# Where a kernel sums its modulation weights, how its weight splits are ranked, and when its attention heads begin

## The chip, the cores and the metric

One NeuronCore of one Trainium2 chip runs the whole program. The metric is device microseconds of one execution, from the first to the last instruction plus what lies around them; smaller is better. PE is the matmul engine, DVE the vector engine, ACT the scalar engine, POOL the general one and SP the engine whose queue issues nearly all DMAs here.

## The reference, cut to what matters

Two transformer blocks run one after the other on 256 tokens of width 2048, all in float32. The second block is modulated: six vectors of 2048 come from a matrix `w_mod` of 2048 x 12288 and one conditioning vector `c`, and they shift, scale and gate the second block only.

```python
def second_block(x, c, w_mod, b_mod, ...):
    mod = silu(c) @ w_mod + b_mod
    sh1, sc1, g1, sh2, sc2, g2 = split(mod, 6)
    h = rmsnorm_2(x, attn_norm_g) * (1.0 + sc1) + sh1
    ...                                       # w_in, two attentions, w_out
    x = x + g1 * (mix @ w_out)
    h = rmsnorm_2(x, mlp_norm_g) * (1.0 + sc2) + sh2
    u = relu(h @ w_ff1)
    x = x + g2 * ((u * u) @ w_ff2)
    return rmsnorm_2(x, final_norm_g)
```

The first block (`first_block`) is: norm, `w_in`, three kinds of attention heads, `w_out`; norm, a gated feed-forward net with `w_gate`, `w_up`, `w_down`; norm, and a small gated embedding with `w_ple_gate` and `w_ple_proj`. Nothing of it needs `mod`.

## The kernel before

**Stages.** `build` runs them in order: `mixer1` (w_in and the heads of the first block), `out_proj1` (w_out), `conv_ffn` (gate, up, down, then `ple_values`), `ple`, `mixer2` and `out_proj2` (second block's attention), `mlp2` (ff1 and ff2). In the profiled execution DVE's first weight split of `out_proj1` is at about 352 us, of `conv_ffn` at 448, of `ple` at 1170, of `mixer2` at 1251 and of `mlp2` at 1492; the first three are called the first three stages below.

**Weights.** Each weight matrix is streamed once in blocks of 512 KB. `prep` (L283) loads a block into `raw` (4 buffers), makes `whi`, its rounded part, on ACT (L291) and `wlo`, the remainder, on DVE (L292); `whi` and `wlo` have 3 buffers each. Every product is three matmuls: `linear` (L328 to L330) has the weights moving, `linear_t` (L370 to L372) has them standing still. After each block `tick` (L260) lets waiting pieces of other work go on: `spawn` starts a generator, whose `yield n` means "go on n blocks later"; `jobs` holds attention heads that begin as ticks allow.

**Modulation sums.** `w_mod` has 96 rows of 128 outputs, each summed in two halves, so 192 halves. `mod_half` (L920) loads half a row block, 512 KB, into one of two `wmod` buffers and multiplies and sums it on DVE (L930) with `cact`, the activated vector `c`. The load may not be issued ahead of the newest weight load (`issue_after`). `tick` calls it `mod_rate` times per block: 0.36 after the first block column of w_in. `mod_upto(80)` at the end of `conv_ffn` issues what is left of the first 160 halves at once. The last 32 halves, which make `g2`, are done in `mlp2`: there a second `mod_open` loads and activates `c` again, the rate is 1.0, and `mod_upto(96)` and `mod_row` (a transpose, a store and a spread back over the partitions) stand ahead of the fifth ff1 chunk.

**Order of the work.** The program is traced once; a list scheduler then fixes the order of each engine's instructions by priority (the place in the trace) and by readiness in its own cost model. On the chip each engine runs its instructions in that fixed order and waits at each for its inputs. `high_priority()` gives what is traced inside it rank 0, ahead of everything ordinary. `prep` uses it, and so do the last column's evacuation in `ple` (`urgent`) and most of `mod_norm`.

**The two modulated norms.** `mod_norm(i, ss)` (L1104) runs for each half i of the tokens when the last column of `ple` or of `out_proj2` is evacuated: row sums, a power on POOL (`rstd_tile`), four scalings `hn` (L1113), then transposes on PE, scale and shift `z`, and a split into `xt`. Around it, blocks of weights are held in a group: the last blocks of the old matrix run for both halves of the tokens out of tiles such as `whiaaaaa`, the first ones of the new matrix out of `whibbbb` (`seq_out`, `seq_in`). The three single blocks after such a first group take the three `whi`/`wlo` buffers.

**Heads.** In `mixer1`, `qkv` transposes q and k (L653), evacuates them into `qT` (L658, L660) and then appends the heads that are complete to `jobs` (L620). `head` (L768) begins with its score matmuls (L783, L785).

Of the kernel before, what the change touches and what calls it, by code (L numbers as in the profile page):

```python
# [9 lines left out]
F32 = mybir.dt.float32  # L10
# [4 lines left out]
ALU = mybir.AluOpType  # L15
# [6 lines left out]
CW = 512  # L22
# [199 lines left out]
class K:  # L222
    def __init__(self, ctx, tc, a, out):
        self.ctx, self.tc, self.nc, self.a, self.out = ctx, tc, tc.nc, a, out
        self.uid = 0
        self.pend = []
        self.jobs = []
        self.job_every = 0.0
        self.job_acc = 0.0
        self.mod_rate = 0.0  # L230
        self.mod_acc = 0.0
        self.done = set()

    def n(self, s):
        self.uid += 1
# [47 lines left out]
    def prep(self, src, ncol, hold=None, shift=False):  # L283
        nc = self.nc
        pool, n, k = (self.HOLD, len(hold), hold) if hold else (self.W, 3, "")
        with self.tc.high_priority():
            raw = self.t(self.W, [P, 1024], "raw", 4)
            self.wdma = nc.sync.dma_start(raw[:, :ncol], src)
            e, s = (0, 0) if hold else (64, 16 * shift)
            hi, lo = (self.t(pool, [P, 1024 + e], w + k, n, F32R)[:, s:s + 1024] for w in ("whi", "wlo"))  # L290
            nc.scalar.activation(hi[:, :ncol], raw[:, :ncol], AF.Copy)  # L291
            nc.vector.tensor_tensor(lo[:, :ncol], raw[:, :ncol], hi[:, :ncol].bitcast(F32), op=ALU.subtract)  # L292
        return hi, lo

    def load(self, dst, src):
# [11 lines left out]
    def linear(self, xt, name, seq, off, cw, evac, before=None):  # L307


        nc = self.nc  # L310
        left, ps = {}, {}
        for c, b in seq:
            for i in range(2):
                left[c, i] = left.get((c, i), 0) + (len(b) if isinstance(b, tuple) else 1)
        started = set()

        def products(c, b, i, w):
            st = (c, i) not in started
            started.add((c, i))
            left[c, i] -= 1  # L320
            en = left[c, i] == 0
            sl = slice(i * P, (i + 1) * P)
            o = ps[c][i][:, :cw]
            for j in range(2):
                xh, xl = xt(2 * b + j)
                wh = moving(w[0][:, j * cw:(j + 1) * cw])
                wl = moving(w[1][:, j * cw:(j + 1) * cw])
                nc.tensor.matmul(o, xh[:, sl], wh, start=st and j == 0, stop=False)  # L328
                nc.tensor.matmul(o, xh[:, sl], wl, start=False, stop=False)  # L329
                nc.tensor.matmul(o, xl[:, sl], wh, start=False, stop=en and j == 1)  # L330
            return en

        for c, b in seq:
            if c not in ps:
                ps[c] = [self.ps.tile([P, 512], F32, name=self.n("mm"), tag="mm", bufs=4) for _ in range(2)]
            group = b if isinstance(b, tuple) else (b,)
            for b1 in group:
                if before is not None:
                    before(c, b1)
            src = [self.wblock(name, off(c) + b1 * 2 * P * cw, 2, cw) for b1 in group]  # L340
            if len(group) == 1:
                w = self.prep(src[0], 2 * cw)
                for i in range(2):
                    if products(c, b, i, w):
                        evac(c, i, ps[c][i])
                self.tick()
                continue
            ws = [self.prep(x, 2 * cw, ("a" if group[0] else "b") * len(group)) for x in src]
            for i in range(2):
                for n, b1 in enumerate(group):  # L350
                    if products(c, b1, i, ws[n]):
                        evac(c, i, ps[c][i])
                    if n % 2 == 1 or n == len(group) - 1:
                        self.tick()
# [78 lines left out]
    def build(self, stop=None):  # L433
        ctx, tc, nc, a = self.ctx, self.tc, self.nc, self.a
        self.C = self.pool(ctx, "C")
        self.W = self.pool(ctx, "W")
        self.X = self.pool(ctx, "X")
        self.DR = self.pool(ctx, "DR", bass.MemoryType.DRAM)
        self.ps = self.pool(ctx, "ps", bass.MemoryType.PSUM)
        C = self.C  # L440
        self.h = self.t(C, [P, 2, D], "h")
        self.ident = self.t(C, [P, P], "ident")
        self.gains = self.t(C, [P, NG], "gains")
        self.mhalf = self.t(C, [P, 16], "mhalf")
        self.macc = self.t(C, [P, 96, 2], "macc")
        self.modT = self.t(C, [P, 96], "modT")
        self.mhalves = 0
        nc.vector.memset(self.mhalf, -0.5)
        self.G = lambda nme, k=0, w=1: self.gains[:, GOFF[nme] + k:GOFF[nme] + k + w]
        self.mixctx = mixctx = ExitStack()  # L450
        modctx = ExitStack()
        self.modctx = modctx
        Y = self.pool(mixctx, "Y")
        self.mix = self.new_xt(Y, "mix", 8)
        self.MOD = self.pool(modctx, "MOD", side="right")
        with ExitStack() as s:
            self.mixer1(s)
            if stop == "mix":
                self.flush()
                return  # L460
            self.out_proj1()
        mixctx.close()
        if stop == "out1":
            self.flush()
            return
        with ExitStack() as s:
            self.ple_open(s)
            self.conv_ffn()
            if stop == "ffn1":
                self.flush()  # L470
                return
            self.mod_upto(80)
            modctx.close()
            self.holdctx = ExitStack()
            self.HOLD = self.pool(self.holdctx, "HOLD", side="right")
            self.ple()
        if stop == "blk1":
            self.flush()
            return
        with ExitStack() as s:  # L480
            self.mixer2(s)
            if stop == "mix2":
                self.flush()
                return
            self.out_proj2()
        if stop == "out2":
            self.flush()
            return
        self.mlp2()


    def mixer1(self, s):
        nc, a, tc, G = self.nc, self.a, self.tc, self.G
# [175 lines left out]
        for ci, (kind, h0, parts) in enumerate(W_IN_CHUNKS):  # L669
            off = ci * D * CW  # L670
            if kind == "a1":
# [35 lines left out]
                if ci == 0:  # L707
                    def before(c, b):
                        load_x(c, b)
                        if b == 5:  # L710
                            load_h()
                        if b == 7:
                            consts()
                    self.chunk(xg, "w_in", off, KT, CW, evac, before)
                    self.mod_rate = 0.36
                else:
                    self.chunk(xg, "w_in", off, KT, CW, evac)
            elif kind == "a2":
# [48 lines left out]

    def head(self, fam, h, kt, q, k, v, cst):  # L768
        nc, M = self.nc, self.M
        extra = None  # L770
        if fam == "f":
            lh = self.t(M, [P, T], "lh", 2)
# [7 lines left out]
        for i in range(2):  # L780
            o = S[:, 0:P] if i == 0 else S[:, P:384]
            n = P if i == 0 else T
# [10 lines left out]
        hi, lo = self.mix[kt // 4]  # L793
# [309 lines left out]

    def mod_norm(self, i, ss):  # L1104
        nc = self.nc
        rs = self.rstd_tile(ss, i)
        if i == 0:
            self.xn.extend(self.new_xt(self.X, "xt", 8))
        hns = []
        for c in range(4):  # L1110
            hn = self.t(self.HOLD, [P, CW], "hn", self.hnb)
            with self.tc.high_priority():
                nc.vector.tensor_scalar(hn, self.h[:, i, c * CW:(c + 1) * CW], rs, None, op0=ALU.mult)  # L1113
            hns.append(hn)
        yield 2
        sl = slice(i * P, (i + 1) * P)
        for c in range(4):
            pt = self.transpose4(hns[c])
            z = self.t(self.HOLD, [P, 4, P], "z", 2)
            for j in range(4):  # L1120
                k = 4 * c + j
                g, b = self.mgs[:, k:k + 1], self.msh[:, k:k + 1]
# [291 lines left out]
    def mlp2(self):  # L1414
        nc = self.nc
        with ExitStack() as s:
            F = self.pool(s, "F2")
# [3 lines left out]
            ss = self.t(F, [P, 64], "ssf")[:, :2 * NCH + 2].rearrange("p (i c) -> p i c", i=2)  # L1421
# [60 lines left out]
            pend = None  # L1482
            for g in range(4):
                for n in range(4):
                    if g == 1 and n == 0:
                        self.mod_upto(96)
                        self.spawn(self.mod_row([g2], 80, F, 5))
                    ff1(4 * g + n)
                    if g == 0 and n == 0:
                        self.holdctx.close()  # L1490
                        R = self.MOD = self.pool(s, "F3", side="right")
                        self.mod_open(None)
                        g2 = self.t(R, [P, D], "grow")
                        self.mod_rate = 1.0
                    if n == 0 and pend is not None:
                        ff2(pend, False)
                pend = list(range(4 * g, 4 * g + 4))
# [30 lines left out]
```

## Time and profile before

| | us |
|---|---|
| median of 3 runs | 2221.02 |
| lowest and highest | 2218.52, 2226.48 |
| the profiled execution, its own time | 2216.61 |
| span of the profiled execution | 2214.8 |
| granted TensorE clock, mean | 0.995 |

The profile shows one execution: busy time per engine, the waits with what ended them, the chain of work that ended last, and the granted clock, of which 1.00 is 2.4 GHz and 0.5 is 1.2 GHz. A matmul is shown until its modelled end, so PE is at its peak only where the count of matmuls per stretch is at its highest as well: about 360 of the `linear_t` kind or 187 of the `linear` kind in 40 us.

### The profile page before, as it was taken

The numbers are of one execution on the slowest core, as the hardware profiler recorded it, in microseconds if no ns is written. First come the engines' busy times: TensorE is split into PE (matmuls) and PEld (weight loads), VectorE is DVE, ScalarE is ACT, GpSimd is POOL, SyncE is SP. The second block draws the span as 40 slices with busy tenths as digits, with TensorE's granted clock in tenths as the row PEclk, the third lists the DMA queues.
The fourth block names the chain that finished last, engine by engine and source line by source line (L and its number), as shares of the span: only waits on it lengthen the run. The fifth ranks groups of instructions, "written<-read, shape, count | busy, mean of one in ns | idle before, by whom it ended". The sixth has DMA issues, their size and how long they took to land.

```text
span 2214.8 us, 34936 instructions
## 1 busy us (share of the span) xinstructions
PE 2153.0 (97%) x13714; PEld 1966.8 (89%) x13714; DVE 1567.7 (71%) x2329; ACT 1102.2 (50%) x1560; POOL 25.8 (1%) x35
## 2 busy tenths in 40 slices
PE   9999999999999999999999899998989999999998
PEld 7788887899998999989988789888878998998997
DVE  7877776877887687767777766768775555555555
ACT  6655554544454454444455555556434444444444
POOL 0000000000000000000000000000000000000000
PEclk9999999999999999999999999999999999999999
DMA  8665666777777777777778743656886666666664
GB/s 321 226 219 200 209 235 219 250 254 256 272 268 271 271 264 271 271 268 276 269 266 311 246 145 125 185 184 213 300 307 219 200 199 202 199 199 202 200 200 162
DMA packets 147537, 517.82 MB, mean 234 GB/s; under 512 B 17115, under 2 KB 21292, under 8 KB 146860
## 3 DMA queue, kind: packets, MB, share of 16 engines
q1 hardware_dynamic: 147228, 515.58, 68.8%
q8 instruction: 107, 1.75, 0.3%
q14 instruction: 58, 0.48, 0.1%
q10 hardware_dynamic: 144, 0.01, 0.0%
HBM read 513.38 MB, written 2.14 MB: 233 GB/s over the span
## 4 chain that ended last, share of the span: by engine, by line
PE 62%; DMA 7%; issue 6%; DVE 3%; ACT 1%; SPq 0%; POOL 0%; ACTq 0%; POOLq 0%; DVEq 0%
PE mm L372 10%; PE mm L371 10%; PE mm L370 10%; PE mm L330 9%; PE mm L328 9%; PE mm L329 9%; DMA wmod<-in_w_mod 6%; DVE wlo L292 2%; PE aux L392 0%; DMA raw<-in_w_ff 0%; PE aux L760 0%; PE aux L1285 0%; DVE wmod L930 0%; ACT whi L291 0%; PE aux L1236 0%
## 5 line engine op out<-in xcount | busy, mean ns | idle before, releaser
L291 ACT ACTIVATE whi<-raw 128x1024 fp32r<-128x1024 f32 (+1 forms) x746 | 783.2, 1051 | 908.3 <-PE mm L330 495.5
L292 DVE TENSOR_TENSOR wlo<-raw,whi 128x1024 fp32r<-128x1024 f32 (+1 forms) x746 | 902.2, 1215 | 366.9 <-ACT whi L291 365.8
L372 PE MATMUL mm<-xt,wlo 128*128 128x256 f32 x2368 | 653.1, 276 | 8.7 <-DVE wlo L292 8.5
L371 PE MATMUL mm<-xt,whi 128*128 128x256 f32 x2368 | 651.4, 275 | 0.0
L370 PE MATMUL mm<-xt,whi 128*128 128x256 f32 x2368 | 651.3, 275 | 0.0
L372 PEld LDWEIGHTS mm<-xt,wlo 128*128 128x128 f32 x2368 | 454.5, 192 | 11.5 <-DVE wlo L292 11.3
L371 PEld LDWEIGHTS mm<-xt,whi 128*128 128x128 f32 x2368 | 454.6, 192 | 0.2
L370 PEld LDWEIGHTS mm<-xt,whi 128*128 128x128 f32 x2368 | 454.6, 192 | 0.2
L930 DVE SCALAR_TENSOR_TENSOR wmod<-wmod,cact 128x1024 f32<-128x1024 f32 x192 | 234.9, 1223 | 181.0 <-DMA wmod<-in_w_mod 180.3
L329 PE MATMUL mm<-wlo,hid 128*128 128x512 f32 x848 | 322.4, 380 | 1.2 <-DVE wlo L292 1.2
L328 PE MATMUL mm<-whi,hid 128*128 128x512 f32 x848 | 322.5, 380 | 0.0
L330 PE MATMUL mm<-whi,hid 128*128 128x512 f32 x848 | 322.3, 380 | 0.0
L329 PE MATMUL mm<-wlo,xt 128*128 128x512 f32 (+2 forms) x660 | 250.0, 379 | 5.9 <-DVE wlo L292 5.6
L328 PE MATMUL mm<-whi,xt 128*128 128x512 f32 (+2 forms) x660 | 252.5, 383 | 1.2 <-ACT whi L291 1.2
L330 PE MATMUL mm<-whi,xt 128*128 128x512 f32 (+2 forms) x660 | 248.3, 376 | 0.0
L329 PEld LDWEIGHTS mm<-wlo,hid 128*128 128x128 f32 x848 | 160.7, 190 | 25.3 <-DVE wlo L292 2.7
L330 PEld LDWEIGHTS mm<-whi,hid 128*128 128x128 f32 x848 | 160.7, 189 | 22.7
L328 PEld LDWEIGHTS mm<-whi,hid 128*128 128x128 f32 x848 | 160.6, 189 | 22.6 <-DVE t L1438 0.2
L329 PEld LDWEIGHTS mm<-wlo,xt 128*128 128x128 f32 x660 | 124.8, 189 | 27.1 <-DVE wlo L292 11.8
L328 PEld LDWEIGHTS mm<-whi,xt 128*128 128x128 f32 x660 | 124.8, 189 | 17.5 <-ACT whi L291 1.7
L330 PEld LDWEIGHTS mm<-whi,xt 128*128 128x128 f32 x660 | 124.8, 189 | 15.2
L329 PE MATMUL mm<-wlo,mix 128*128 128x512 f32 x244 | 93.0, 381 | 1.9 <-DVE wlo L292 1.9
(349 smaller groups left out, 1790.6 us busy)
## 6 DMA issues: line engine op xcount, KB each, us to landing
raw<-in_w_ff SPq DMA_DIRECT2D x256, 512.0 KB, 4.3
wmod<-in_w_mod SPq DMA_DIRECT2D x192, 512.0 KB, 5.3
raw<-in_w_in SPq DMA_DIRECT2D x120, 512.0 KB, 4.6
raw<-in_w_gate SPq DMA_DIRECT2D x88, 512.0 KB, 4.5
raw<-in_w_up SPq DMA_DIRECT2D x88, 512.0 KB, 4.6
raw<-in_w_down SPq DMA_DIRECT2D x88, 512.0 KB, 4.3
raw<-in_w_out SPq DMA_DIRECT2D x64, 512.0 KB, 3.8
raw<-in_w_pg SPq DMA_DIRECT2D x32, 512.0 KB, 4.8
```

Source lines behind the costliest of these rows:

```text
L291: nc.scalar.activation(hi[:, :ncol], raw[:, :ncol], AF.Copy)
L292: nc.vector.tensor_tensor(lo[:, :ncol], raw[:, :ncol], hi[:, :ncol].bitcast(F32), op=ALU.subtract)
L328: nc.tensor.matmul(o, xh[:, sl], wh, start=st and j == 0, stop=False)
L329: nc.tensor.matmul(o, xh[:, sl], wl, start=False, stop=False)
L330: nc.tensor.matmul(o, xl[:, sl], wh, start=False, stop=en and j == 1)
L370: nc.tensor.matmul(o, hi[:, ws], xh, start=first, stop=False, skip_group_check=True)
L371: nc.tensor.matmul(o, hi[:, ws], xl, start=False, stop=False, skip_group_check=True)
L372: nc.tensor.matmul(o, lo[:, ws], xh, start=False, stop=(b == last and j == 1), skip_group_check=True)
L930: nc.vector.scalar_tensor_tensor(raw, raw, 1.0, self.cact[:, us], op0=ALU.mult, op1=ALU.mult, accum_out=self.macc[:, j, u:u + 1])
```

## The change

Four things are changed. The rate of the modulation sums in the first three stages goes from 0.36 to 0.5 per block, `conv_ffn` ends with `mod_upto(96)`, and everything of them goes out of `mlp2`; `mod_row` for `g2` is started after the first ff1 chunk. The weight splits of `prep` get a rank 2000 places ahead of where they are traced in place of rank 0, and the row sums and the power of `mod_norm` get rank 0. The `wlo` splits of the three single blocks behind a first group are queued on DVE behind the last `hn` of half 0. And `head` yields once ahead of its score matmuls.

```diff
     def prep(self, src, ncol, hold=None, shift=False):
-        with self.tc.high_priority():
+        with self.tc.high_priority(offset=min(2000, self.tc.cur_priority)):
             ...
-            nc.vector.tensor_tensor(lo[:, :ncol], raw[:, :ncol], hi[:, :ncol].bitcast(F32), op=ALU.subtract)
+            with self.tc.issue_after(self.behind.ins) if self.behind is not None else nullcontext():
+                nc.vector.tensor_tensor(lo[:, :ncol], raw[:, :ncol], hi[:, :ncol].bitcast(F32), op=ALU.subtract)
     def linear(...):
+        ring = 0
             if len(group) == 1:
+                self.behind = self.normed if ring > 0 else None
+                ring -= 1
                 w = self.prep(src[0], 2 * cw)
+                self.behind = None
             ...
             ws = [self.prep(x, 2 * cw, ("a" if group[0] else "b") * len(group)) for x in src]
+            ring = 0 if group[0] else 3
     def build(...):
-            self.mod_upto(80)
+            self.mod_upto(96)
     def mixer1(...):
-                    self.mod_rate = 0.36
+                    self.mod_rate = 0.5
     def head(self, fam, h, kt, q, k, v, cst):
         nc, M = self.nc, self.M
+        yield 1
     def mod_norm(self, i, ss):
-        rs = self.rstd_tile(ss, i)
+        with self.tc.high_priority():
+            rs = self.rstd_tile(ss, i)
             ...
-                nc.vector.tensor_scalar(hn, self.h[:, i, c * CW:(c + 1) * CW], rs, None, op0=ALU.mult)
+                op = nc.vector.tensor_scalar(hn, self.h[:, i, c * CW:(c + 1) * CW], rs, None, op0=ALU.mult)
+            if i == 0:
+                self.normed = op
     def mlp2(self):
-                    if g == 1 and n == 0:
-                        self.mod_upto(96)
-                        self.spawn(self.mod_row([g2], 80, F, 5))
                     ff1(4 * g + n)
                     if g == 0 and n == 0:
                         self.holdctx.close()
-                        R = self.MOD = self.pool(s, "F3", side="right")
-                        self.mod_open(None)
+                        R = self.pool(s, "F3", side="right")
                         g2 = self.t(R, [P, D], "grow")
-                        self.mod_rate = 1.0
+                        self.spawn(self.mod_row([g2], 80, F, 3))
```

## Rows read from the trace of the kernel before

**Rows 1.** The page, part 1: busy us, share of the span, instructions.
```profile
PE 2153.0 (97%) x13714; PEld 1966.8 (89%) x13714; DVE 1567.7 (71%) x2329; ACT 1102.2 (50%) x1560; POOL 25.8 (1%) x35
```
**Rows 2.** Stretches: us, busy of PE, PEld, DVE, ACT, POOL, clock, DMA, GB/s.
```profile
448.00:1160.00 712.00, 708.78 (x5332) 678.10 (x5331) 540.57 (x685) 336.08 (x370) 0.70 (x1) 1.00 0.77 267
1160.00:1250.00 90.00, 86.31 (x396) 72.92 (x396) 73.46 (x96) 50.28 (x66) 1.51 (x1) 1.00 0.87 302
...
1478.00:1524.00 46.00, 41.49 (x204) 35.29 (x203) 36.43 (x58) 28.78 (x47) 1.10 (x2) 1.00 0.53 175
1524.00:1660.00 136.00, 122.34 (x913) 113.91 (x912) 103.02 (x130) 59.53 (x68) 0.00 (x0) 0.99 0.87 305
1660.00:2200.00 540.00, 540.00 (x3523) 502.17 (x3523) 316.68 (x318) 243.94 (x261) 0.00 (x0) 1.00 0.62 199
```
**Rows 3.** Waits of PE, 1523 to 1680: us in total, times, longest.
```profile
PE mm L372 <- DVE wlo L292: 7.5, 9, 1.5
PE aux L950 <- DVE modT L942: 3.6, 1, 3.6
PE mm L329 <- DVE wlo L292: 1.2, 3, 0.7
```
**Rows 4.** Stretches around three stops of PE, columns as in rows 2.
```profile
212.00:220.00 8.00, 5.18 (x20) 4.51 (x21) 5.36 (x20) 1.94 (x6) 0.00 (x0) 0.79 0.53 191
1260.00:1272.00 12.00, 7.34 (x29) 6.73 (x30) 8.28 (x18) 5.71 (x12) 1.02 (x2) 0.72 0.46 155
1652.00:1662.00 10.00, 6.58 (x24) 5.44 (x25) 6.43 (x10) 3.96 (x7) 0.00 (x0) 0.83 0.81 283
```
**Rows 5.** DVE by line, 448 to 1160: busy us, mean ns, idle before.
```profile
L292 DVE TENSOR_TENSOR wlo<-raw,whi 128x1024 fp32r<-128x1024 f32 x265 | 321.5, 1222 | 78.2 <-ACT whi L291 77.9
L930 DVE SCALAR_TENSOR_TENSOR wmod<-wmod,cact 128x1024 f32<-128x1024 f32 x96 | 117.4, 1223 | 91.6 <-DMA wmod<-in_w_mod 91.2
```
**Rows 6.** The same, 1524 to 1660.
```profile
L292 DVE TENSOR_TENSOR wlo<-raw,whi 128x1024 fp32r<-128x1024 f32 x44 | 53.3, 1220 | 2.4 <-ACT whi L291 2.3
L930 DVE SCALAR_TENSOR_TENSOR wmod<-wmod,cact 128x1024 f32<-128x1024 f32 x32 | 39.2, 1225 | 29.5 <-DMA wmod<-in_w_mod 29.5
```
**Rows 7.** The same, 1160 to 1250.
```profile
L292 DVE TENSOR_TENSOR wlo<-raw,whi 128x1024 fp32r<-128x1024 f32 x30 | 36.2, 1219 | 2.4 <-ACT whi L291 2.4
L930 DVE SCALAR_TENSOR_TENSOR wmod<-wmod,cact 128x1024 f32<-128x1024 f32 x19 | 23.2, 1223 | 13.9 <-DMA wmod<-in_w_mod 13.8
```
**Rows 8.** Waits of PE, 1165 to 1262.
```profile
PE mm L329 <- DVE wlo L292: 2.3, 4, 1.5
```
**Rows 9.** Loads of wmod, issue to landing: 448 to 1160, then 1524 to 1660.
```profile
DMA to landing us min/median/max: 4.3/5.1/7.5
...
DMA to landing us min/median/max: 4.6/5.6/7.5
```
**Rows 10.** Timeline, ple to mixer2: start, us, engine, line; idle and its ender.
```profile
1258.06 0.67 ACT L1072 ACTIVATE t<-mm,rs 128x512 f32<-128x512 f32 x1
...
1259.32 0.68 DVE L1073 TENSOR_TENSOR t<-t,pe 128x512 f32<-128x512 f32 x1
1259.93 1.22 DVE L292 TENSOR_TENSOR wlo<-raw,whi 128x1024 fp32r<-128x1024 f32 x1
1261.06 0.68 DVE L1074 TENSOR_TENSOR h<-h,t 128x512 f32<-128x512 f32 x1
...
1264.66 3.65 PE L392 MATMUL aux<-ident,hn 128*128 128x128 f32 x16 [5.01 <-DVE hn L1113]
```
**Rows 11.** Timeline, out_proj2 to mlp2.
```profile
1497.99 2.51 DVE L292 TENSOR_TENSOR wlo<-raw,whi 128x1024 fp32r<-128x1024 f32 x2 [0.82 <-ACT whi L291]
...
1504.33 1.94 PE L392 MATMUL aux<-ident,hn 128*128 128x128 f32 x16 [3.31 <-DVE hn L1113]
```
**Rows 12.** Waits of PE, 110 to 380.
```profile
PE aux L783 <- ACT qT L660: 5.0, 2, 3.4
PE mm L329 <- DVE wlo L292: 2.5, 4, 1.3
```

More of the change, by code (lines that the diff above doesn't have):

```diff
@@ L232, in __init__ @@
         self.done = set()
+        self.behind = self.normed = None
     def n(self, s):
```

## The prediction, made before the changed kernel was run

> **What bounds the kernel now.** I read the page first, then the stretches by stage, then the waits of PE in each stretch, and last the timelines where PE stops. PE is busy for 97% of the span [rows 1], and the stretches show where the rest is: from 1660 to 2200 PE has no idle time at all, from 448 to 1160 it loses 3.2 us of 712, but from 1524 to 1660 it loses 13.7 of 136, from 1160 to 1250 3.7 of 90, and from 1478 to 1524 4.5 of 46 [rows 2]. So the kernel is bound by its matmuls, and a change can only give back PE's stops: those where the modulation sums are dense, those at the two modulated norms, and a few in the first stage. What it can cost is new stops, most of all between 448 and 1160, where a full PE sits beside a DVE that is itself nearly full.
>
> **The change part by part.** The sums are made against the profiled execution (2216.61 us, of which the span is 2214.8), which is 4.4 us below the median of the three runs (2221.02); I apply the differences to the median.
>
> *How many halves move.* At one tick per block the first three stages have, behind w_in's first column, 96 ticks of w_in, 32 of w_out, 176 of gate and up, 88 of down and 4 of `ple_values`: 396. At 0.36 that is 142 halves; the trace has 96 of them from 448 on [rows 5]. The other 18 of the first 160 come in a burst from 1160 on (19 there with one that straddles the edge, rows 7), and 32 lie behind 1524 [rows 6]. At 0.5 all 192 are used up after 384 ticks, some 12 ticks ahead of the end: 64 by the end of w_out (18 more than now) and 128 in `conv_ffn` (some 33 more). The burst and the 32 go. The number of loads and of DVE operations stays as it is but for the second load and activation of `c`.
>
> *A. What `mlp2` gives back.* From 1523 to 1680 PE waits 7.5 and 1.2 us for `wlo` and once 3.6 us for `modT`, the transpose of `mod_row` that needs the very last half [rows 3]. Behind that stop the granted clock is 0.83 over 10 us, so 1.7 us went at half clock [rows 4]. With the sums done long before, `mod_row` finds its inputs ready; its transpose, its store and its row load on SP move some four ff1 chunks ahead, into PE's and SP's ordinary stream. The cover for it is the stretch as it runs behind 1660: no idle time of PE at 199 GB/s [rows 2]. A = 8.7 + 3.6 + 1.7 = 14.0; bounds 12.3 (no clock) to 15.4 (all of the 13.7, and the clock).
>
> *B. The burst.* From 1165 to 1262 PE waits 2.3 us for `wlo` of the 3.7 that it loses up to 1250 [rows 2, 8]. B = 2.3, bounds 1 to 3.7.
>
> *C. The norm behind `ple`.* PE stands for 5.01 us until half 0's `hn` is there, and the transposes then run at a low clock, 0.72 over 12 us, which is 3.4 us lost [rows 4, 10]. In the chain to `hn`, ACT's `t` ends at 1258.73, but DVE's `t` begins at 1259.32, and a `wlo` of 1.13 us lies between it and `h` [rows 10]. These `wlo`, and a third one behind `h`, go behind `hn`: 0.6 + 1.1 + about 0.2 = 1.9 us. What is queued behind `hn` now are three splits, and behind these the raw buffers that they free and SP's next weight load; the PE work that needs them stands behind half 0's transposes and the new held group, so I count nobody who waits. The matmuls of half 1 follow the transposes, so part of the lost clock comes back as well; I take half of 3.4. C = 1.9 + 1.7 = 3.6. Bounds: 0 (the stop only moves to the next late input) and 7.2, if the rank also lets ACT's `t` pass the `whi` of 1.06 us ahead of it and the clock stays up.
>
> *D. The norm ahead of `mlp2`.* Here the two splits up to 1500.5 stand straight ahead of the chain, and PE stops for 3.31 us [rows 11]. But the same DVE must do them before half 1 is through: that evacuation isn't `urgent`, so the moved splits (rank 2000 places ahead) stand in front of half 1's `t` and `h`. Half 0 gains, half 1 doesn't, and DVE is busy for 36 of 46 us there [rows 2]. D = 1, bounds -2 (single blocks that PE now uses as filling come too late) to 3.3.
>
> *E. Heads.* PE waits 5.0 us in two stops for `qT` ahead of the scores, the longer one 3.4 [rows 12]; around that one the clock is 0.79 over 8 us, 1.7 us lost [rows 4]. One block later (712 us for 265 blocks, 2.7 us each, rows 2 and 5) `qT` is there in the one and nearly so in the other. The lag of a block at the end is covered: the last heads are first needed 14 blocks into w_out and are done after about 9. The loads of the alibi rows on SP move with the heads and keep their lead over the softmax. E = 5.5, bounds 0 (another wait takes the place) to 6.7.
>
> *F. What `conv_ffn` pays.* A half costs DVE 1.22 us and 0.95 us of waiting for its load (91.2 us for 96, rows 5). 33 more: 33 x 2.17 = 72 us. DVE's spare time there is what it waits for ACT ahead of `wlo`, 77.9 us [rows 5]. It just fits, with nothing left for uneven stretches. For the price of not fitting I take PE's loss per split against halves per split: 0.36 halves (96 to 265) cost 1.0 us or less, 0.004 us per split; 0.54 (19 to 35, the five held splits among them) cost 2.3 us, 0.066; 0.73 (32 to 44) cost 8.7, 0.20 [rows 3, 5 to 8]. The change comes to 128 to 265, 0.48. On a straight line between the first two that is 0.045 per split, 12 us; since the spare time only just runs out there, I take 7. Bounds 0 and 17.5 (0.066 on all 265).
>
> A rule stands against this caution. The rows: the two dense stretches moved 302 and 305 GB/s [rows 2], a load of a half landed after 5.6 us in place of 5.1 [rows 9], and PE lost time in both. At 0.5 halves per block, 199 x 1.5 = 299 GB/s are asked for. The Trainium skill, DMA: Bandwidth & Descriptors, section Specifications, puts the HBM limit of a core at about 358 GB/s; by that there is room, the loads would not be late, F would be nothing, and the time that of the free case below. The rows decide for me: what bound those stretches was not the rate but the in-order wait of DVE for each load.
>
> *G. The first stages.* 18 halves more; splits were late for 2.5 us now between 110 and 380 [rows 12]. Doubling that is 2.5, and w_out a little: G = 3, bounds 0 and 8.
>
> Sum: 14.0 + 2.3 + 3.6 + 1.0 + 5.5 = 26.4 gained, 7 + 3 = 10 paid, net 16.4: the profiled execution would take 2200.2, the median 2204.6. I predict **2204.5 us**.
>
> **The rivals.**
> 1. *The sums are free*: F and G are nothing, and C and E come near their upper ends: 26.4 + 3 = 29, so 2192. For it: the spare time of DVE covers the 72 us. Against it: it does so only on average, and both denser stretches lost PE time. Chance 0.17.
> 2. *Rank, order and heads do nothing*: the orders were fixed by a model in which loads land early, so `whi` on ACT still stands ahead of the evacuation, and another input is as late as `qT`. Then A + B - F - G = 14.0 + 2.3 - 10 = 6.3, so 2214.7. For it: ACT's `t` itself came late at 1258.06 [rows 10]. Against it: the three splits in the chain are moved by an edge, not by rank. Chance 0.15.
> 3. *DVE tips over in `conv_ffn`, and the kernel gets slower*: each added half makes DVE stand at a load while the splits behind it wait, for the whole stage. At the price of the stretch behind 1524, 0.20 us per split, F is 265 x 0.20 = 53, and the net is 26.4 - 53 - 3 = -30: 2251. It decides from (26.4 - 3) / 265 = 0.09 us per split on. For it: gate and up carry more evacuation on DVE than the dense stretches. Against it: there are a third fewer halves per split than there. Chance 0.13, half of it in milder form near 2225 to 2235.
>
> **How the numbers follow.** The forecast (net 8 to 24, so 2197 to 2213) has 0.55. What a measurement of this kernel can tell from no change is about 0.3%, 6.7 us: faster is below 2214.4, slower above 2227.7. The forecast gives 0.52 of faster and 0.03 of the same; the free case 0.17 faster; rival 2 lies on the edge, 0.07 and 0.08; rival 3 gives 0.04 of the same and 0.09 slower. Together 0.76, 0.15, 0.09. The range goes from the free case, 2190, to where rival 3 begins, 2221; about 0.1 lies outside on either side.
>
> **What would show it.** Right: no L930 behind 1160 and no stop of PE behind the second norm up to the end of ff2's first pass; no wait of L783 for `qT`; `hn` of half 0 about 2 us sooner behind its held group, with the three `wlo` behind it; in `conv_ffn` 128 halves, DVE's wait ahead of `wlo` for ACT shrunk from 78 us to near nothing, and PE behind `wlo` for some 7 us. Wrong: PE waiting for `wlo` in `conv_ffn` for over 20 us (F), the stop ahead of half 0's transposes as long as now (C), a new stop of several us between half 0 and half 1 ahead of ff1 (D), or scores that wait for something else (E).

## The result and the profile after

The changed kernel took **2195.36 us** (median of 4 runs, 2194.37 to 2196.09) beside 2220.33 us for the kernel before on the same chip: ratio 0.988, interval 0.9859 to 0.9901. The forecast was 2204.5 with a range of 2190 to 2221. The profiled execution took 2196.09 us, 20.5 less than the one before in span (2194.3 against 2214.8).

Every kernel here has the same 12,624 matmuls of weights (`mm`), so the end of the n-th of them can be compared in any two traces. The table gives the length of six stages in the trace of before, and by how many us they are longer or shorter in the other traces. It is worked out from the end of the last product of each stage; the labels e1 to e12 are the experiments below.

| us | w_in | w_out | conv_ffn | ple | mixer2 to first ff1 | mlp2, sums' part |
|---|---|---|---|---|---|---|
| products up to | 1,248 | 1,632 | 6,912 | 7,344 | 8,208 | 9,360 |
| before, length | 355.1 | 97.1 | 708.4 | 109.4 | 260.9 | 189.9 |
| after | -1.4 | -1.9 | +5.8 | -6.2 | +3.2 | -20.0 |
| after, again (e7) | -3.2 | +1.1 | +7.6 | -6.7 | +3.3 | -20.0 |
| sums alone (e1) | +9.5 | +1.8 | +8.4 | -6.5 | 0.0 | -20.0 |
| heads alone (e2) | -1.4 | +2.1 | +0.4 | +1.0 | +0.8 | -2.0 |
| norms alone (e3) | +3.5 | +0.5 | +0.4 | +0.5 | +2.2 | -2.8 |
| late sums left out (e4) | +3.4 | +2.2 | -0.9 | +0.9 | +2.0 | -20.0 |
| sums and heads (e5) | -2.9 | -1.5 | +8.6 | -6.3 | +2.1 | -20.0 |
| without the edges (e6) | -1.4 | +1.5 | +10.6 | -4.8 | -0.3 | -20.0 |
| two more steps (e8) | -2.7 | +1.3 | +5.0 | -8.3 | -1.0 | -20.0 |
| first of these alone (e11) | -2.2 | -0.6 | +8.1 | -8.3 | +1.0 | -20.0 |
| second alone (e12) | -2.1 | -1.4 | +12.4 | -5.7 | +1.3 | -20.0 |
| sums without loads (e9) | -3.3 | -1.5 | +5.1 | -6.9 | +3.4 | -20.0 |
| sums cut short (e10) | -9.8 | +1.4 | -2.6 | -7.2 | +2.7 | -20.0 |

Stages that an edit doesn't touch differ by up to 3 us from trace to trace (e2 and e3 in the last column), and w_in of e1 to e4 holds 2 to 4 us of slower start, so single entries below that are noise. The base matters too, in the last column most of all: against e2 and e3, which make the late sums too, the changed kernel is 17.9 and 17.1 us shorter there.

The page's part 1 of the changed kernel, which answers rows 1:

```profile
PE 2149.0 (98%) x13714; PEld 1967.2 (90%) x13714; DVE 1560.4 (71%) x2327; ACT 1100.2 (50%) x1557; POOL 26.0 (1%) x35
```

and its stretches, with the columns of rows 2: `conv_ffn`, `ple`, the norm ahead of `mlp2`, the part of `mlp2` that held the sums, and the rest.

```profile
447.00:1163.00 716.00, 710.16 (x5324) 676.49 (x5323) 572.02 (x752) 335.09 (x369) 0.70 (x1) 1.00 0.83 289
1163.00:1257.00 94.00, 91.64 (x428) 79.72 (x426) 58.98 (x60) 57.68 (x75) 1.78 (x1) 1.00 0.68 217
1480.00:1522.00 42.00, 36.96 (x170) 32.01 (x169) 30.01 (x51) 24.53 (x42) 1.10 (x2) 0.92 0.51 158
1522.00:1648.00 126.00, 125.91 (x959) 120.86 (x959) 73.30 (x73) 60.88 (x69) 0.00 (x0) 1.00 0.67 208
1648.00:2180.00 532.00, 532.00 (x3486) 495.19 (x3485) 309.99 (x310) 240.91 (x258) 0.00 (x0) 1.00 0.63 198
```

In `mlp2` PE is now busy for 125.91 of 126 us (122.34 of 136 in rows 2), at 208 GB/s in place of 305. `conv_ffn` carries the load instead: 289 GB/s against 267, and PE loses 5.84 us of 716. The norm ahead of `mlp2` still costs PE 5 of 42 us, and the clock there is 0.92.

DVE by line in `conv_ffn` (busy us, mean ns, idle before and what ended it), which answers rows 5:

```profile
L294 DVE TENSOR_TENSOR wlo<-raw,whi 128x1024 fp32r<-128x1024 f32 x266 | 318.3, 1219 | 17.1 <-ACT whi L292 16.7
L938 DVE SCALAR_TENSOR_TENSOR wmod<-wmod,cact 128x1024 f32<-128x1024 f32 x127 | 155.3, 1223 | 125.3 <-DMA wmod<-in_w_mod 125.2
```

127 halves stand there and 65 ahead of it, where 128 and 64 were counted. The spare time that the forecast set against them, DVE's wait for ACT ahead of `wlo`, is used up: 16.7 us in place of 77.9. The last half begins at 1131.3 us, so from `ple` on there is none.

### The profile page after: what moved, and what is told of

Its sections match the earlier page's. It is cut to its first block, busy times and chain, and to the rows that moved or that the text cites. A ratio compares the mean times of both kernels' runs of the same rounds, so it can differ in the third digit from the quotient of the medians.

```text
span 2194.3 us, 34907 instructions
## 1 busy us (share of the span) xinstructions
PE 2149.0 (98%) x13714; PEld 1967.2 (90%) x13714; DVE 1560.4 (71%) x2327; ACT 1100.2 (50%) x1557; POOL 26.0 (1%) x35
## 4 chain that ended last, share of the span: by engine, by line
PE 74%; DMA 11%; DVE 9%; issue 3%; ACT 2%; POOL 1%; SPq 0%; DVEq 0%; ACTq 0%; POOLq 0%
PE mm L332 12%; PE mm L333 12%; PE mm L331 12%; PE mm L379 11%; PE mm L378 11%; PE mm L377 11%; DMA wmod<-in_w_mod 9%; DVE wlo L294 5%; DVE wmod L938 1%; ACT whi L292 1%; DMA raw<-in_w_in 1%; PE aux L399 1%; DMA raw<-in_w_ff 0%; PE aux L767 0%; PE aux L842 0%
## 5 line engine op out<-in xcount | busy, mean ns | idle before, releaser
L331 PE MATMUL mm<-whi,mix 128*128 128x512 f32 x244 | 94.9, 390 | 0.0
```

## The experiments

Ratios are against the kernel before on the same chip. The changed kernel ran twice: 0.988, and 0.9899 (0.9881 to 0.9916) as e7, so ratios from different sets of runs agree to about 0.2%.

### e1: the sums alone

```diff
-                    self.mod_rate = 0.36
+                    self.mod_rate = 0.5
...
-            self.mod_upto(80)
+            self.mod_upto(96)
...
-                    if g == 1 and n == 0:
-                        self.mod_upto(96)
-                        self.spawn(self.mod_row([g2], 80, F, 5))
...
-                        R = self.MOD = self.pool(s, "F3", side="right")
-                        self.mod_open(None)
-                        self.mod_rate = 1.0
+                        R = self.pool(s, "F3", side="right")
...
+                        self.spawn(self.mod_row([g2], 80, F, 3))
```

> Only the modulation sums are moved: 0.5 per block in the first three stages, nothing of them in mlp2; ranks, edges and heads as before. If the trace after is read rightly (theory P: what PE loses is told by its pace, matmuls per stretch, and the sums account for nearly all of the gain), the stretch behind the start of mlp2 gets some 20 us shorter, the burst 5.5 us, conv_ffn 6 us longer and w_in with w_out about 3 us longer: net 16 to 18 us under the kernel before. Rival I (idle time of PE tells all): 14 + 2.3 - 10, so 6 us under, and the rest of the 25 us comes from the norms and the heads.

Measured: 2211.3 us, 0.9952 (0.9934 to 0.9971), a gain of 10 us, between the two expectations. The table shows why neither held: `mlp2` gave its full 20.0 and `conv_ffn` cost 8.4, but w_in cost another 9.5 (2.4 of it in the start). PE's waits from 110 to 390 us:

```profile
PE aux L783 <- ACT qT L660: 9.8, 3, 3.8
PE aux L883 <- DVE t L878: 1.6, 2, 1.1
PE mm L329 <- DVE wlo L292: 1.3, 2, 0.7
```

and the clock around the three stops at the scores (stretch, then as in rows 2):

```profile
218.00:226.00 8.00, 5.87 (x23) 5.13 (x24) 6.01 (x24) 2.91 (x9) 0.00 (x0) 0.79 0.46 173
300.00:308.00 8.00, 4.53 (x16) 3.87 (x16) 5.88 (x18) 2.53 (x10) 0.00 (x0) 0.79 0.83 298
380.00:388.00 8.00, 5.31 (x14) 4.31 (x15) 5.88 (x18) 2.45 (x9) 0.00 (x0) 0.60 0.61 241
```

The price of denser sums in the first stages wasn't more waiting for `wlo`; it was that `qT`, which stands in the same queues, came later: three stops of 9.8 us in place of two of 5.0 [rows 12], each followed by a stretch at half clock.

### e2: the later heads alone

```diff
     def head(self, fam, h, kt, q, k, v, cst):
         nc, M = self.nc, self.M
+        yield 1
```

> Only the heads begin one block later. Theory P: the two stops of PE at the scores (5.0 us and 1.7 us of clock) shrink by 3 to 6 us, so 3 to 6 us under before. Rival: another wait takes their place (the changed kernel still shows one stop of 1.9 us at the scores), 0 to 2 us.

Measured: 2217.37 us, 0.9979 (0.9964 to 0.9993): 4 us of gain, as expected.

### e3: the norms alone (ranks and edges)

The changed kernel with the sums and the heads put back.

> Only the ranks (weight splits 2000 places ahead, row sums and power at rank 0) and the edge of the three splits behind the last scaling of half 0, at both norms; sums and heads as before. Theory P: the norm behind ple gains 0.5 to 2 us, the one ahead of mlp2 loses 3 (two stops of 2.5 us, each followed by 3.4 us at half clock, for one of 3.3), so 1 to 3 us slower than before. Rival (as predicted): 4 to 5 us faster.

Measured: 2224.03 us, 1.0014 (1.0000 to 1.0029). The norms' part alone gains nothing, as expected here, where the prediction had 4.6 us for it.

### e4: the late sums left out

```diff
-                    if g == 1 and n == 0:
-                        self.mod_upto(96)
-                        self.spawn(self.mod_row([g2], 80, F, 5))
...
-                        self.mod_rate = 1.0
+                        self.spawn(self.mod_row([g2], 64, F, 3))
```

> The last 32 halves are left out altogether, and g2 is made from the rows of another section, so that the result of the last stage isn't the reference's; all else as before (0.36, burst of 18). It measures what the 32 halves, the second activation of c and the late transpose cost in mlp2. Theory P (pace): 20 us under before. Rival I (idle time and clock): 14 to 15.4 us under.

Measured: 2202.52 us, 0.991 (0.9891 to 0.993), 18.9 us less; the same stretch of `mlp2` is 20.0 us shorter, just as after the change. So the whole gain of the changed kernel in `mlp2` is the absence of these 32 halves, with the second activation of `c` and the late transpose that go with them. It is 17 to 20 us, by the execution that it is set against, and not the 14 that the trace's waits and its clock add up to.

### e5 to e7: sums with heads; without the edges; the change again

The first is the kernel before with the diffs of e1 and e2. The second is the changed kernel with

```diff
-            ring = 0 if group[0] else 3
+            ring = 0
```

> The kernel before with the sums of the change and its later heads, and without the ranks and edges of the norms. Sums alone were worth 10 us and heads alone 4 us. Theory J (the parts hang together: with 0.5 of a half per tick VectorE and ScalarE are so full in the stage of w_in that the heads' old place costs PE two to three times what it cost at 0.36, so that the later heads are worth 8 to 13 us beside the sums, and the norms' part is worth nothing or costs 2 to 3 us): 20 to 27 us faster than before, 2194 to 2201 us, as fast as the changed kernel or faster by up to 3 us. Rival K (the parts add up, and what is missing between their sum of 11 us and the change's 25 us lies in the norms' part once the late sums are gone): 14 us faster, about 2207 us.

> The changed kernel without the two edges (no weight split waits for half 0's modulated norms; the smaller ranks of the splits stay). Theory J: in the changed kernel the three moved splits stand ahead of half 1's chain ahead of mlp2 and cost PE 2.2 us more than before; without the edges the kernel is 1 to 4 us faster than the changed one, and TensorE doesn't stop between the transposes of mlp2's first group for more than 3 us in all. Rival K: the edges carry the missing part, so that it is 3 to 10 us slower than the changed kernel.

> The changed kernel as it is, for its time on the chip on which the variants run: 23 to 27 us faster than before by both theories.

Measured: sums and heads 2197.33 us, 0.9891 (0.9874 to 0.9907); without the edges 2199.24, 0.9899 (0.9881 to 0.9918); the changed kernel 2199.39, 0.9899. The three can't be told apart. Theory J holds: alone the sums give 10 us and the heads 4, together they give 25, and the norms' part adds nothing beside them. The table shows where the parts hang together: w_in and w_out change by +11.3 with the sums alone, by +0.7 with the heads alone (over 2 us of each in the start), and by -4.4 with both. The scores' stop with both (PE's waits, 110 to 380 us) is a fifth of that of e1:

```profile
PE aux L784 <- ACT qT L660: 1.9, 1, 1.9
```

Theory J's second half, that the edges cost 1 to 4 us, isn't shown: e6 has the same time.

### e8, e11 and e12: two more steps at the norms

```diff
+            with self.tc.issue_after(self.squared.ins) if self.behind is not None else nullcontext():
-            nc.scalar.activation(hi[:, :ncol], raw[:, :ncol], AF.Copy)
+                nc.scalar.activation(hi[:, :ncol], raw[:, :ncol], AF.Copy)
...
-            self.linear(self.xt_get(self.mix), "w_out2", seq, lambda c: c * D * CW, CW, evac, lambda c, b: self.need_mix(b))
+            self.linear(self.xt_get(self.mix), "w_out2", seq, lambda c: c * D * CW, CW, self.urgent(evac), lambda c, b: self.need_mix(b))
```

`squared` is the last sum of squares (L419) of half 0. e8 has both steps, e11 the first, e12 the second.

> The changed kernel with two more steps on the same chain: the three moved splits are held back on ScalarE too (their copy to the high part goes behind half 0's last sum of squares), and out_proj2's results are added to h with high priority. If what holds half 0's chain ahead of mlp2 is ScalarE waiting for a weight load ahead of the sum of squares (2.04 us in the trace of the changed kernel), the first of the two stops there (2.53 us, then 3.4 us at the lower clock) goes, and the kernel is 2 to 5 us faster than the changed one. If the order on PE sets these stops (its transposes are placed too early for any chain), it is within 1.5 us of the changed one; the three weights that come later by the step can also stop PE behind the transposes, and then it is 1 to 3 us slower.

> The changed kernel with the copies to the high part of the three moved splits behind half 0's last sum of squares, and out_proj2's additions to h at their old rank: one of the two steps of the run in which both were made, which was 4.9 us faster than the changed kernel. If ScalarE's wait for a weight load ahead of the sum of squares is what holds half 0's chain, this step carries most of it: 3 to 5 us faster than the changed kernel, both stops ahead of mlp2 under 1 us. If the order of the additions to h on VectorE is what holds it, 0 to 2 us faster, and the stop at half 1's transposes stays at 2 to 2.5 us.

> The changed kernel with out_proj2's additions to h at high priority, and ScalarE's copies where the changed kernel has them: the other of the two steps. If the order of the additions to h on VectorE behind the moved splits is what holds half 1's chain, the second stop (2.50 us and 3.4 us at the lower clock) goes and the kernel is 2 to 4 us faster than the changed one; if ScalarE's wait is all, 0 to 1 us.

Measured: both 2194.49 us, 0.9876 (0.9858 to 0.9894), 4.9 us below the changed kernel in the same set of runs (e7); the first step 2197.63, 0.989 (0.9872 to 0.9908); the second 2199.55, 0.9902 (0.9885 to 0.9919). The intervals of all three overlap that of the changed kernel, so no step is shown by the times; the traces show the mechanism. The changed kernel ahead of `mlp2`, timeline (start, us, engine, line; idle before and its ender):

```profile
1495.70 1.06 ACT L292 ACTIVATE whi<-raw 128x1024 fp32r<-128x1024 f32 x1 [2.04 <-DMA raw<-in_w_ff]
1496.67 0.61 ACT L419 ACTIVATE junk<-h 128x512 bf16<-128x512 f32 x1
...
1499.11 3.40 PE L399 MATMUL aux<-ident,hn 128*128 128x128 f32 x16 [2.53 <-DVE hn L1122]
...
1500.06 1.22 DVE L294 TENSOR_TENSOR wlo<-raw,whi 128x1024 fp32r<-128x1024 f32 x1
...
1505.67 1.22 DVE L294 TENSOR_TENSOR wlo<-raw,whi 128x1024 fp32r<-128x1024 f32 x1
...
1508.05 0.69 DVE L1403 TENSOR_TENSOR t<-mm,cT 128x512 f32<-128x512 f32 x1
...
1509.25 0.69 DVE L1404 TENSOR_TENSOR h<-h,t 128x512 f32<-128x512 f32 x1
...
1512.34 3.06 PE L399 MATMUL aux<-ident,hn 128*128 128x128 f32 x16 [2.50 <-DVE hn L1122]
```

Half 0's `h` was done at 1494.79, but ACT stood 2.04 us at a `whi` whose weight hadn't landed, and the sum of squares behind it began at 1496.67. The moved splits, three from 1500.06 to 1506.89, then stood ahead of half 1's `t` and `h`. The same place with both steps:

```profile
1493.88 0.63 ACT L420 ACTIVATE junk<-h 128x512 bf16<-128x512 f32 x1 [4.29 <-DVE h L1407]
...
1496.35 1.94 PE L400 MATMUL aux<-ident,hn 128*128 128x128 f32 x16 [0.78 <-DVE hn L1125]
...
1500.92 0.68 DVE L1407 TENSOR_TENSOR h<-h,t 128x512 f32<-128x512 f32 x1
...
1506.33 1.97 PE L400 MATMUL aux<-ident,hn 128*128 128x128 f32 x16 [0.26 <-DVE hn L1125]
```

The sum of squares follows `h` at once, the stops fall from 2.53 and 2.50 us to 0.78 and 0.26, the transposes take 1.94 in place of 3.40 us, and against the changed kernel the stage from mixer2 to the first ff1 is 4.2 us shorter and `ple` 2.1. With the first step alone (e11) it is 2.2 and 2.1 us, with the second alone (e12) 1.9 and -0.5. These are single traces; four with the changed kernel's order at this place (after, e7, e9, e10) lie within 0.7 us of each other in the first stage and within 1.1 in `ple`. The stops tell more than the sums: with the first step alone half 0's is 0.77 us and half 1's is gone, as expected of it, but a wait of 0.86 us for `xt` between them is followed by a dip of the clock; with the second alone half 1's falls to 0.26 and half 0's stays at 2.16. So ACT's wait was what held half 0.

### e9 and e10: what the sums cost in `conv_ffn`

e9 reads the resident `cact` in place of a loaded `wmod`:

```diff
-        with self.tc.issue_after(self.wdma.ins):
-            nc.sync.dma_start(raw, self.a["w_mod"][j * P:(j + 1) * P, us])
-        nc.vector.scalar_tensor_tensor(raw, raw, 1.0, self.cact[:, us], op0=ALU.mult, op1=ALU.mult,
+        nc.vector.scalar_tensor_tensor(raw, self.cact[:, us], 1.0, self.cact[:, us], op0=ALU.mult, op1=ALU.mult,
```

e10 keeps the loads and cuts the operation short:

```diff
-        nc.vector.scalar_tensor_tensor(raw, raw, 1.0, self.cact[:, us], op0=ALU.mult, op1=ALU.mult,
+        nc.vector.scalar_tensor_tensor(raw[:, :64], raw[:, :64], 1.0, self.cact[:, u * 1024:u * 1024 + 64], op0=ALU.mult, op1=ALU.mult,
```

> The changed kernel with the 96 halves' weight loads left out (VectorE reads the resident cact rows in place of the loaded tile, so g1, g2 and the other modulation rows aren't those of the reference). VectorE still does each of the 96 operations at its full length, but waits for no load. Theory W (what the earlier sums cost in the stages of w_in and conv_ffn is VectorE standing in order behind a load that hasn't landed, and the bytes' share of the transfers): conv_ffn takes about as long as before the change or less, 704 to 709 us against 714 from w_out's last product to that of the last down block, and the kernel is 4 to 9 us faster than the changed one. Theory V (the cost is the operations' own time on VectorE, which the weight splits need): conv_ffn stays within 2 us of the changed kernel's, and the kernel within 2 us.

> The changed kernel with all its loads, but with VectorE's operation of each of the 96 halves on 64 of its 1024 columns (so the modulation rows leave out most of their sum). Theory W: each operation still stands behind its load, so conv_ffn gets back under half of its 5.8 us, and the kernel is 0 to 3 us faster than the changed one. Theory V: about 1 us of VectorE less for each of 64 halves in conv_ffn gives back the 5.8 us, and the kernel is 4 to 9 us faster than the changed one.

Measured: without the loads 2194.49 us, 0.9878 (0.986 to 0.9895), no different from the changed kernel, `conv_ffn` +5.1 us against before; with short operations 2180.69, 0.9812 (0.979 to 0.9833), 15 to 19 us below the changed kernel's two medians, more than the 4 to 9 that theory V gave. Against the profiled changed kernel it gains 8.4 us in `conv_ffn` (-2.6 in place of +5.8) and as much again in w_in (-9.8 in place of -1.4); w_out gives 3.3 of it back. In `conv_ffn` theory V holds, and W falls. With short operations DVE still stands 74.6 us at the loads (DVE by line, `conv_ffn`),

```profile
L294 DVE TENSOR_TENSOR wlo<-raw,whi 128x1024 fp32r<-128x1024 f32 x268 | 327.8, 1223 | 174.3 <-ACT whi L292 173.2
L938 DVE SCALAR_TENSOR_TENSOR wmod<-wmod,cact 128x64 f32<-128x64 f32 x126 | 28.1, 223 | 75.3 <-DMA wmod<-in_w_mod 74.6
```

and no wait of PE for a split is left there. Counted by PE's pace, the time from one matmul to the next where nothing is late (a split is late where its first matmul, right behind another product, ends over 0.1 us later than that), the changed kernel has 16 late splits in `conv_ffn` that cost 6.8 us, before has 2 that cost 1.6, and this run none. Its only wait of PE is this:

```profile
PE aux L977 <- DVE wmod L938: 1.2, 1, 1.2
```

e9 did more than it was meant to: without a load to wait for, all 192 operations ran between 62 and 609 us. That splits `conv_ffn` into a stretch with 61 of them, 0.75 per split (61 to 81) where the changed kernel has 0.48, and one with none (columns as in rows 2):

```profile
447.00:672.00 225.00, 220.67 (x1929) 216.86 (x1929) 206.50 (x305) 107.64 (x122) 1.07 (x1) 1.00 0.56 190
672.00:1163.00 491.00, 491.00 (x3403) 461.63 (x3403) 297.97 (x323) 228.53 (x250) 0.00 (x0) 1.00 0.58 198
```

At 190 GB/s and with no load to wait for, the first part (products 1,633 to 3,552) still takes 7.7 us longer than in e10. The timeline of PE shows one delay of it,

```profile
501.20 0.28 PE L377 MATMUL mm<-xt,whi 128*128 128x256 f32 x1
501.32 0.28 PE L378 MATMUL mm<-xt,whi 128*128 128x256 f32 x1
501.72 0.38 PE L379 MATMUL mm<-xt,wlo 128*128 128x256 f32 x1
```

and that of DVE its cause:

```profile
499.29 1.23 DVE L936 SCALAR_TENSOR_TENSOR wmod<-cact 128x1024 f32<-128x1024 f32 x1
500.43 0.09 DVE L936 DVE_READ_ACCUMULATOR wmod<-cact 128x1 f32 x1
500.43 1.23 DVE L294 TENSOR_TENSOR wlo<-raw,whi 128x1024 fp32r<-128x1024 f32 x1
```

The modulation operation runs straight ahead of a split, the split ends at 501.66, and its first matmul begins 0.40 us behind the one before it, where 0.11 is the pace, and itself takes 0.38 in place of 0.28: 0.39 us lost. The trace counts 0.13 of that as idle time, too little for a bracket in the row. 17 late splits like this one make up the 7.7 us. So operations without a load to wait for do make splits late; since they stand denser here, e9 doesn't tell what the waits add at the changed kernel's own density.

In w_in the two causes aren't told apart: e9 has 97 full operations up to 354 us there in place of 50, none with a load to wait for, and is 1.9 us shorter than the changed kernel, and e10, which keeps the waits, is 8.4 us shorter.

## Why the prediction was right, point by point

The mechanism (bound by the matmuls, with stops where DVE is crowded) and the sign held, and the median came 9.1 us below the point. Two of the prediction's own signs of being wrong came true, the stop ahead of half 0's transposes (C) and the new one at half 1's (D), and of the waits for `qT` one of 1.9 us is left (E). The terms below make 4.1 of it (16.4 of net gain predicted, 20.5 in the span); 4.4 is that the profiled execution of before lay that far below its median, and 0.7 that the profiled one of after lay above its own; these two are scatter of single executions and no part of the working.

**A, `mlp2`: 14.0 predicted, 20.0 measured** (e4 too; 17.1 and 17.9 against e3 and e2). This is the term that was mis-sized, above its upper bound of 15.4. Product by product, in the trace of before, 16 late splits cost 13.1 us, two waits of PE's transposes for `t` 1.3, the stop for `modT` 3.9 and the clock behind it 1.6. Clock and `modT` were right (1.7 and 3.6); the splits were read as 8.7 us from PE's waits [rows 3], and `t` was left out. Each visible wait on a split hid some 0.27 us more, and four late splits were not in the list. One of the visible ones, in PE's timeline of the kernel before:

```profile
1560.23 0.28 PE L371 MATMUL mm<-xt,whi 128*128 128x256 f32 x1
1561.83 0.38 PE L372 MATMUL mm<-xt,wlo 128*128 128x256 f32 x1 [1.32 <-DVE wlo L292]
1562.04 0.28 PE L370 MATMUL mm<-xt,whi 128*128 128x256 f32 x1
```

From the matmul ahead of the late one to the matmul behind it there are 1.81 us, where two steps of the pace are 0.22: 1.59 lost for 1.32 shown. The Trainium skill, Perfetto Trace Analysis, section Identifying the Most-Contended Engine, says that the busy share of matmuls is not a good measure of how close a kernel is to roofline, its peak, because they are pipelined. The trace agrees: 13.7 us idle [rows 2] stood for 20.0 lost.

**B and C, `ple`: 5.9 predicted, 6.2 to 6.7 measured**, but not in those parts. Up to the held group the gain is 5.6 us (B, 2.3 predicted, bound 3.7): again late splits cost more than their waits, seven of them 4.3 us, and all went. C gained 0.6 in place of 3.6. The chain from ACT's `t` to the transposes did get shorter by 1.8 us, 1.9 forecast, from 6.60 [rows 10] to 4.83:

```profile
1254.26 0.38 PE L332 MATMUL mm<-wloaaaaa,xt 128*128 128x512 f32 x1
1254.57 0.67 ACT L1080 ACTIVATE t<-mm,rs 128x512 f32<-128x512 f32 x1
...
1256.00 0.69 DVE L1082 TENSOR_TENSOR h<-h,t 128x512 f32<-128x512 f32 x1
...
1259.40 3.65 PE L399 MATMUL aux<-ident,hn 128*128 128x128 f32 x16 [4.76 <-DVE hn L1122]
...
1260.36 1.21 DVE L294 TENSOR_TENSOR wlo<-raw,whi 128x1024 fp32r<-128x1024 f32 x1
```

The splits stand behind `hn`, as meant. But PE's own order changed too: nine products of the held group now stand behind half 0's transposes (these come behind product 7,331 in place of 7,340). The edges did that and not the ranks, since e6, which has the ranks alone, has them behind 7,340 still and e3 behind 7,331. So the stop begins 0.07 us behind the start of `t`, where it was 1.59 [rows 10]. The cover shrank by nearly as much as the chain, and the stop is 4.76 us in place of 5.01, with the same dip of the clock. The failed step is that PE's place of the transposes was taken as fixed. The sum of B and C fitted by luck, B's excess covering what C lacked.

**D, the norm ahead of `mlp2`: 1.0 predicted, a loss of 3.2 in the profiled run**, beyond the bound of -2, and 0.0 to 2.1 in the traces with the norms of before (e1, e2, e4, e5), so 1 to 3 us of it belong to the norms' part, and to its edges, since the ranks alone (e6) have -0.3. The direction given for half 1, splits ahead of its `t` and `h`, is what the timeline shows. What the forecast left out is the clock. In the trace of before the one stop of 3.31 us had no dip behind it, but that isn't the rule: in e1, e2, e4 and e5 the same stop (3.35, 3.68, 4.57 and 4.51 us) has one each time. In the changed kernel two stops of 2.5 us have one each. Before and e1 (stretches behind the stop, as in rows 2, and e1's stop):

```profile
1504.00:1509.00 5.00, 3.53 (x22) 2.84 (x23) 4.90 (x12) 3.61 (x9) 0.00 (x0) 1.00 0.01 6
...
1517.00:1522.00 5.00, 4.39 (x20) 3.76 (x21) 4.91 (x12) 3.35 (x8) 0.00 (x0) 0.66 0.09 35
...
1517.60 3.04 PE L392 MATMUL aux<-ident,hn 128*128 128x128 f32 x16 [3.35 <-DVE hn L1113]
```

and the changed kernel:

```profile
1499.00:1503.00 4.00, 3.89 (x19) 3.81 (x20) 3.88 (x9) 2.58 (x6) 0.00 (x0) 0.57 0.15 32
1512.00:1517.00 5.00, 4.66 (x21) 3.99 (x22) 4.32 (x11) 3.68 (x9) 0.00 (x0) 0.66 0.01 2
```

**E and G, w_in and w_out: 2.5 net predicted, 3.3 measured**, and from 4.4 gained to nothing in the six other traces with both at full length (e5 to e8, e11, e12). The sum was right by luck, its two terms weren't: taken one at a time the heads give 4 us in time (5.5 predicted) and the sums cost 9 in w_in and w_out beyond the start (3 predicted, bound 8), most of it at the scores (e1). The prediction priced the denser sums by the waits for `wlo` alone and kept the heads' gain as it was at 0.36. They hang together: denser sums make `qT` later, which makes the later heads worth more.

**F, `conv_ffn`: 7 predicted, 5.8 measured** in the profiled run; 5.0 to 12.4 in the seven other traces with sums at 0.5 and full operations (e1, e5 to e8, e11, e12), 8.4 in the middle. The size was right. The reason given, DVE's in-order wait for each load, fell as the cause by itself: with the loads kept and the operation cut short the cost is gone (e10), and with the loads gone and the operation kept it isn't (e9, at a higher density). What the waits add beside full operations isn't shown. What makes a split late is 1.2 us of another operation just ahead of it on DVE, and with 127 of these to 266 splits ACT's `whi` is no longer what the split waits for.

**The rate of the loads.** `conv_ffn` ran at 289 GB/s and was not free; e10, at 288 to 293 GB/s, was. So the rate was no bound in either, and what the free case missed was DVE's own time. The Trainium skill, DMA: Bandwidth & Descriptors, section Specifications, puts the HBM limit of a core at about 358 GB/s. Both runs lie below that, and no run here shows the limit itself; that below it the sums would be free was the prediction's own step, and it did not hold.

**The rivals.** The free case came closer in time than the forecast (2192, 3.4 us off), by luck: F and G weren't nothing, A was larger. DVE didn't tip over: 5.8 us on 265 splits is 0.022 a split, a quarter of the 0.09 from which the kernel would have been slower, and the 12.4 of e12 is 0.047. That ranks, order and heads do nothing is half true: ranks and edges do nothing that a time shows (e3, e5, e6), the heads do.

## What to carry to other kernels

Price a crowded stretch by where the same matmul ends with and without the crowd, not by adding up the idle time shown: late inputs cost more than their waits. Before a stop of a few us is priced, look at the same stop in several executions: the clock behind it differs. Two edits that share a queue are priced together; here one was worth 10 us, the other 4, and both 25. An order that is changed for one engine changes the others' too, so a shorter chain gains only what the waiting engine's new place leaves of it.

## What was not expected of the hardware

A late operand costs PE some 0.27 us beyond the idle time in the trace: 0.40 us between matmuls that are 0.11 apart, with 0.13 counted idle; 0.35 lost where 0.08 was shown, and 0.87 where 0.60 was (all in e9). Of the 0.27, 0.17 is that a matmul is shown for 0.28 us though they begin 0.11 apart, and 0.10 that the late one is shown for 0.38. The clock's dip behind a stop isn't set by the stop's length alone: behind 3.31 us ahead of `mlp2` in the kernel before there was none, behind 3.35 at the same place in e1 there were 3.4 us at the lower level, worked out from 0.66 over 5; behind 2.53 and 2.50 in the changed one there were each time some 3.4 us at the lower level (1.2 GHz), worked out from 0.57 over 4 us and 0.66 over 5; behind stops of 0.78 and 0.26 in e8 there was none. What decides it wasn't tried.
